# One weight load for a run of matmuls on the same selector, and the diagonal block group by group

One Trainium2 chip, one core. The metric is device time of one execution in microseconds (us), lower is better. "Before" and "after" are the two kernels; a load is a LDWEIGHTS instruction, a burst is PE's work on one strip.

## The reference

```python
B, H, W = 4, 4224, 4224                      # x: fp32, 285 MB
def reference(x):
    ps = np.cumsum(np.cumsum(x, axis=1), axis=2)
    diag = np.diagonal(ps, axis1=1, axis2=2)
    return np.cumsum(diag, axis=1).astype(np.float32)   # (4, 4224)
```

Only the diagonal of the 2D prefix sum is wanted, so each input value has to be read once and added into a few sums.

## The kernel before

Each batch is read in strips of 768 rows, cast to bf16 by the transfer, into three buffers. On a strip, TensorE (PE) sums columns right of the diagonal block, VectorE (DVE) masks the diagonal block and sums rows, ScalarE (ACT) sums the rest of the rows. PE's column sums all go into one tile `d` with a row for each group of 384 columns. A slice of `sel` (128 x 11, one column of ones) as weights, called a selector here, picks the row. A fold (`fold_in`) adds slices of a strip into one tile, with the identity as weights.

```python
def load_rows(o, b, r0):                       # a strip: 12.98 MB of fp32
    nc.gpsimd.dma_start(out=o, in_=x[b, r0 : r0 + f * P, :]...)
def matmul(o, lhsT, rhs, start=False):
    nc.tensor.matmul(o, lhsT=lhsT, rhs=rhs, start=start, stop=False, skip_group_check=True)
def fold_in(o, src, c0, c1, w, start=False):
    for c in range(c0, c1, w):
        matmul(o, ident_h, src[..., c : c + w], start=start and c == c0)
...
def columns(j, lo, hi, rhs):
    k = row_of(j)
    matmul(d[:, lo:hi], sel[:, NG - 1 - k : 2 * NG - 1 - k], rhs, start=first[0])
    first[0] = False
def add_up(strip, f, r0, acc, um, wp=0, ws=None):
    for j in range(g + nw, NG):                # right of the diagonal block
        for q in range(f):
            columns(j, 0, GW, strip[:, q, j * GW : (j + 1) * GW])
    ...
    nc.vector.tensor_mul(out=mu, in0=block, in1=um)
    nc.vector.tensor_sub(out=block, in0=block, in1=mu)
    for q in range(f):                         # the diagonal block: two selectors in turn
        for h in range(nw):
            columns(g + h, 0, GW, mu[:, q, h * GW : (h + 1) * GW])
        if ws > wp:
            act_sum(acc[:, q, 0:1], strip[:, q, wp:ws])
    row_sums(acc[:, :, 1], strip[:, :, ws:hi])
```

The end of the last batch is cut into small transfers, so that little work is left when the last of them lands.

## Time and profile before

| | before |
|---|---|
| time, median of 3 runs | 668.15 us (667.28 to 669.49) |
| span of the profiled run | 665.7 us |
| read from HBM | 285.47 MB, 429 GB/s |
| PE matmuls / weight loads | 981 / 981 |
| busy PE / weight loads / DVE / ACT | 204.5 / 97.8 / 334.6 / 140.3 us |

Busy times of weight loads overlap those of the matmuls (they have a row of their own, PEld). The groups concerned, from the page's part 5 (line, engine, operation, output<-inputs, shapes, count | busy us, mean ns | idle before and what ended it):

```profile
L208 PE MATMUL d<-strip,sel 128*11 128x384 bf16 x603 | 138.7, 403 | 377.7 <-DMA strip<-in_x_dram 377.7
...
L208 PEld LDWEIGHTS <-sel 128*11 128x11 bf16 x849 | 86.2, 102 | 522.3 <-issue 479.3
```

The other lines of before are in the prediction.

### The profile page before, as it was taken

The page shows a single profiled execution, that of the slowest core. Times are in us where ns is not written, and L with a number is a line of the kernel's source. Part 1 is how long each engine was busy: PE and PEld are TensorE (multiplying, and loading weights), DVE is VectorE, ACT ScalarE, POOL GpSimd, SP SyncE. Part 2 cuts the span into 40 slices and gives each one's busy share as a digit, 9 for nine tenths or more (in the row PEclk, how much of TensorE's full clock was granted, in tenths as well). Part 3 has the DMA queues.
Part 4 walks back from the last instruction along what each step waited for, and adds up shares of the span by engine and source line. Part 5 has one row for each costly group of instructions (what it writes and reads, how often), then busy time and mean ns, then how long its engine had stood idle before and what let it go on. Part 6 is the DMA issues. An engine that isn't in the chain of part 4 may idle for free.

```text
span 665.7 us, 2562 instructions
## 1 busy us (share of the span) xinstructions
PE 204.5 (31%) x981; PEld 97.8 (15%) x981; DVE 334.6 (50%) x165; ACT 140.3 (21%) x226; POOL 31.3 (5%) x59
## 2 busy tenths in 40 slices
PE   0081522403117143130221623504032263250427
PEld 0030211101003021110110311202011031120203
DVE  3161625456916153454782524436288343352767
ACT  0001120406300103040630020304063002030436
POOL 7000000000000000000000000000000000001000
PEclk9995857656558585675755957666565586766758
DMA  9999999999999999999999999999999999999998
GB/s 203 219 219 219 219 218 218 219 212 207 220 221 216 219 219 215 219 215 216 212 219 222 218 215 219 216 216 218 216 213 219 221 213 220 216 216 218 218 207 162
DMA packets 7670, 143.23 MB, mean 215 GB/s; under 512 B 702, under 2 KB 1002, under 8 KB 2154
## 3 DMA queue, kind: packets, MB, share of 16 engines
q0 software_dynamic: 7296, 142.47, 99.9%
q1 hardware_dynamic: 362, 0.61, 0.3%
q8 instruction: 7, 0.11, 0.1%
q14 instruction: 5, 0.04, 0.0%
HBM read 285.47 MB, written 0.07 MB: 429 GB/s over the span
## 4 chain that ended last, share of the span: by engine, by line
DVE 47%; another core or an unknown queue 45%; DMA 5%; PE 2%; issue 1%; DVEq 0%; POOLq 0%
DVE acc L230 29%; DVE mu L320 8%; DVE strip L321 8%; DMA strip<-in_x_dram 5%; PE d L208 1%; DVE c L436 1%; PE fold L208 1%; DVE pu L230 0%; DVE c L250 0%; DVE rows L360 0%; DVE acc L335 0%; PE carry_ps L208 0%; DVE pair L239 0%; PE fin L208 0%
## 5 line engine op out<-in xcount | busy, mean ns | idle before, releaser
L208 PE MATMUL d<-strip,sel 128*11 128x384 bf16 x603 | 138.7, 403 | 377.7 <-DMA strip<-in_x_dram 377.7
L225 ACT ACTIVATE dump<-strip 128x416 bf16<-128x416 bf16 (+8 forms) x112 | 128.4, 1146 | 522.0 <-DMA strip<-in_x_dram 519.3
L320 DVE TENSOR_TENSOR mu<-strip,um 128x4608 bf16<-128x4608 bf16 (+1 forms) x24 | 52.4, 2183 | 307.1 <-DMA strip<-in_x_dram 307.0
L230 DVE TENSOR_REDUCE acc<-strip 128x6 f32<-128x4608 bf16 (+6 forms) x23 | 196.0, 8523 | 0.8
L208 PEld LDWEIGHTS <-sel 128*11 128x11 bf16 x849 | 86.2, 102 | 522.3 <-issue 479.3
L208 PE MATMUL d<-mu,sel 128*11 128x384 bf16 x243 | 49.1, 355 | 45.8 <-DVE mu L320 45.8
L321 DVE TENSOR_TENSOR strip<-strip,mu 128x4608 bf16<-128x4608 bf16 (+1 forms) x24 | 52.4, 2183 | 1.0
L76 POOL DMA_DIRECT2D strip<-in_x_dram x24 | 16.4, 686 | 543.0 <-DVE acc L230 281.7
L225 ACT ACTIVATION_READ_ACCUMULATOR dump<-strip 128x1 f32 x112 | 20.9, 186 | 0.0
L208 PE MATMUL d<-ident,rows 128*11 128x128 f32 x24 | 5.2, 379 | 16.8 <-DVE rows L369 16.8
L208 PE MATMUL fold<-strip,ident_h 128*128 128x480 bf16 x8 | 3.4, 598 | 10.7 <-DMA strip<-in_x_dram 10.7
L208 PE MATMUL d<-halves,rows 128*11 128x64 f32 x48 | 5.5, 296 | 0.0
L94 DVE MEMSET um<- 128x4608 bf16 (+1 forms) x2 | 4.9, 2458 | 1.1 <-issue 1.1
L208 PEld LDWEIGHTS d<-ident,rows 128*11 128x11 f32 x24 | 2.6, 119 | 18.5 <-DVE rows L369 11.7
L95 POOL TENSOR_SCALAR_AFFINE_SELECT um<-um 128x4608 bf16<-128x4608 bf16 (+1 forms) x2 | 5.2, 2611 | 2.4 <-DVE um L94 2.4
L208 PEld LDWEIGHTS d<-halves,rows 128*11 128x11 f32 x48 | 5.1, 134 | 1.5 <-issue 1.5
L230 DVE TENSOR_REDUCE pu<-d 11x1 f32<-11x384 f32 x4 | 2.2, 546 | 5.2 <-PE d L208 5.2
L436 DVE TENSOR_TENSOR_SCAN c<-ones_row,carry,c 11x384 f32<-11x384 f32 x4 | 4.0, 1005 | 0.1
L436 DVE TENSOR_TENSOR_SCAN c<-ones_row,carry,d 11x384 f32<-11x384 f32 x4 | 4.0, 1000 | 0.1
L409 POOL DMA_DIRECT2D strip<-in_x_dram x5 | 2.7, 557 | 26.4 <-DMA strip<-in_x_dram 26.4
L208 PEld LDWEIGHTS <-ident_h 128*128 128x128 bf16 x14 | 1.6, 119 | 13.8 <-issue 13.5
L230 DVE TENSOR_REDUCE parts<-strip 128x3 f32<-128x3072 bf16 x1 | 3.4, 3353 | 0.0
(87 smaller groups left out, 37.2 us busy)
## 6 DMA issues: line engine op xcount, KB each, us to landing
strip<-in_x_dram POOLq DMA_DIRECT2D x19, 6336.0 KB, 76.7
strip<-in_x_dram POOLq DMA_DIRECT2D x5, 3168.0 KB, 59.9
strip<-in_x_dram POOLq DMA_DIRECT2D x1, 1080.0 KB, 49.9
strip<-in_x_dram POOLq DMA_DIRECT2D x1, 768.0 KB, 52.9
strip<-in_x_dram POOLq DMA_DIRECT2D x3, 256.0 KB, 54.1
head<-in_x_dram SPq DMA_DIRECT2D x1, 528.0 KB, 4.0
strip<-in_x_dram POOLq DMA_DIRECT2D x1, 192.0 KB, 43.2
strip<-in_x_dram POOLq DMA_DIRECT2D x1, 64.0 KB, 28.6
```

Of the source, the lines that this page charges most:

```text
L76: nc.gpsimd.dma_start(out=o, in_=x[b, r0 : r0 + f * P, :].rearrange("(p f) w -> p f w", f=f))
L94: nc.vector.memset(um, 1.0)
L95: nc.gpsimd.affine_select(out=um, in_=um, compare_op=ALU.is_gt, fill=0.0, base=0, pattern=[[-1, f], [1, f * P]], channel_multiplier=-f,)
L208: nc.tensor.matmul(o, lhsT=lhsT, rhs=rhs, start=start, stop=False, skip_group_check=True)
L225: nc.scalar.activation(out=dump[:, :w], in_=src, func=ACT.Copy, accum_out=acc)
L230: nc.vector.reduce_sum(out=acc, in_=src, axis=AX.X)
L320: nc.vector.tensor_mul(out=mu, in0=block, in1=um)
L321: nc.vector.tensor_sub(out=block, in0=block, in1=mu)
L409: nc.gpsimd.dma_start(out=part_b[:, sb, c0:c1], in_=x[b, r0 : r0 + R, :TB].rearrange("r (k c) -> r k c", k=4)[:, :, c0:c1],)
L436: nc.vector.tensor_tensor_scan(out=c12[:, i, :], data0=ones_row, data1=src, initial=carry[:, i : i + 1], op0=ALU.mult, op1=ALU.add,)
```

## The change

The intent: in a run of matmuls on one selector, or on the identity in the folds, only the first loads the weights, and the others are issued as an instruction that says `ldweights=False`. To have such runs in the diagonal block too, its loops are exchanged: all rows of one column group, then all of the next.

```diff
+    def matmul_on(o, lhsT, rhs):
+        te = nc.tensor
+        te.add_instruction(mybir.InstMatmult(
+            start_tensor_calc=False, stop_tensor_calc=False,
+            tile_position=(0, 0), tile_size=(P, P if lhsT.shape[-1] > 64 else 32),
+            bass_skip_group_check=True, ldweights=False,
+            ...  # name, engine, ins=[rhs, lhsT], outs=[o]
+        ))
     def fold_in(o, src, c0, c1, w, start=False):
         for c in range(c0, c1, w):
-            matmul(o, ident_h, src[..., c : c + w], start=start and c == c0)
+            if c == c0:
+                matmul(o, ident_h, src[..., c : c + w], start=start)
+            else:
+                matmul_on(o, ident_h, src[..., c : c + w])
-        def columns(j, lo, hi, rhs):
+        def columns(j, lo, hi, rhs, same=False):
+            ...
+            if same:
+                matmul_on(d[:, lo:hi], lhsT, rhs)
+                return
@@ add_up @@
-                    columns(j, 0, GW, strip[:, q, j * GW : (j + 1) * GW])
+                    columns(j, 0, GW, strip[:, q, j * GW : (j + 1) * GW], q > 0)
+            for h in range(nw):
+                for q in range(f):
+                    columns(g + h, 0, GW, mu[:, q, h * GW : (h + 1) * GW], q > 0)
             for q in range(f):
-                for h in range(nw):
-                    columns(g + h, 0, GW, mu[:, q, h * GW : (h + 1) * GW])
```

The three matmuls of the last 128 x 128 block get the same treatment (`h > 0`).

More of the change, by code (lines that the diff above doesn't have):

```diff
@@ L210, in matmul @@
         )
+    def matmul_on(o, lhsT, rhs):
+        te = nc.tensor
+        te.add_instruction(
+            mybir.InstMatmult(
+                start_tensor_calc=False,
+                stop_tensor_calc=False,
+                tile_position=(0, 0),
+                tile_size=(P, P if lhsT.shape[-1] > 64 else 32),
+                bass_skip_group_check=True,
+                ldweights=False,
+                name=nc.get_next_instruction_name(),
+                engine=te.engine,
+                ins=[
+                    te.lower_ap(rhs, opt=False),
+                    te.lower_ap(lhsT, opt=False, for_matmul_weights=True),
+                ],
+                outs=[te.lower_ap(o)],
+            )
+        )
     weights4_h = consts.tile([P, P], BF16, name="weights4_h")
@@ L297, in row_of @@
             return (j + t0) % NG
-        def columns(j, lo, hi, rhs):
+        def columns(j, lo, hi, rhs, same=False):
             k = row_of(j)
-            matmul(
-                d[:, lo:hi], sel[:, NG - 1 - k : 2 * NG - 1 - k], rhs, start=first[0]
-            )
+            lhsT = sel[:, NG - 1 - k : 2 * NG - 1 - k]
+            if same:
+                matmul_on(d[:, lo:hi], lhsT, rhs)
+                return
+            matmul(d[:, lo:hi], lhsT, rhs, start=first[0])
             first[0] = False
@@ L353 @@
                 for h in range(3):
-                    columns(LG, h * P, GW, hmu[:, h, : GW - h * P])
+                    columns(LG, h * P, GW, hmu[:, h, : GW - h * P], h > 0)
         a6 = acc6[:, :ns]
```

## The prediction

> **What bounds the kernel now.** I began with the page: busy shares (part 1), the slices (part 2), the bytes (part 3), the chain (part 4).
>
> ```profile
> PE 204.5 (31%) x981; PEld 97.8 (15%) x981; DVE 334.6 (50%) x165; ACT 140.3 (21%) x226; POOL 31.3 (5%) x59
> ...
> PEclk9995857656558585675755957666565586766758
> DMA  9999999999999999999999999999999999999998
> GB/s 203 219 219 219 219 218 218 219 212 207 220 221 216 219 219 215 219 215 216 212 219 222 218 215 219 216 216 218 216 213 219 221 213 220 216 216 218 218 207 162
> ...
> HBM read 285.47 MB, written 0.07 MB: 429 GB/s over the span
> ```
>
> No compute engine is busy more than half of the span. The DMA row is 9 from the first slice to the last, and the rate lies near 217 GB/s throughout (the cast from fp32 to bf16 halves what is counted there; read from HBM it is 429 GB/s). So the kernel is a stream of 285 MB, with a short piece of work behind it. One strip of 768 rows is 768 x 4224 x 4 bytes = 12.98 MB, at 429 GB/s an estimated 30.2 us. The chain of waits shows this beat: the first DVE instruction on a strip starts at 34.8, 64.8, 95.2, 125.1 and 155.0 us. The chain's 45% for "another core or an unknown queue" are the 11 to 20 us gaps between the strips' DVE work, and in the timeline they end with a DMA landing. I read them as waiting for data.
>
> Two places could still be sensitive to PE. The first is the issue of a strip's DMA, which waits until PE, DVE and ACT are through with the old strip in that buffer. The timeline at the end of the first batch, where buffers come free latest:
>
> ```profile
> 174.25 0.71 POOL L76 DMA_DIRECT2D strip<-in_x_dram  x1 [31.27 <-ACT dump L225]
> 183.12 0.71 POOL L76 DMA_DIRECT2D strip<-in_x_dram  x1 [8.16 <-issue]
> ...
> 199.99 2.56 DVE L320 TENSOR_TENSOR mu<-strip,um 128x4608 bf16<-128x4608 bf16 x1 [11.63 <-DMA strip<-in_x_dram]
> ```
>
> The strip that lands at 200 was issued at 142.28. While it streams, the next two are queued at 174.25 and 183.12, so the queue has some 26 us of stock (200 - 174) in its leanest moment. A full strip takes 76.7 us (median) from issue to landing against a beat of 30: it sits in line some 46 us. An issue that comes a few us sooner or later shifts no landing. PE is the last releaser for only 4 of the strip issues (112.2 us of POOL's waiting), and POOL waiting costs nothing while the queue is stocked.
>
> The second place is the end, in the timeline:
>
> ```profile
> 655.80 0.55 DVE L230 TENSOR_REDUCE pu<-d 11x1 f32<-11x384 f32 x1 [0.53 <-PE d L208]
> 661.52 0.46 DVE L239 SCALAR_TENSOR_TENSOR pair<-strip 128x288 f32<-128x288 bf16 x1 [0.85 <-DMA strip<-in_x_dram]
> 662.46 0.39 DVE L239 SCALAR_TENSOR_TENSOR pair<-strip 128x224 f32<-128x224 bf16 x1 [0.15 <-DMA strip<-in_x_dram]
> 662.92 0.50 PE L208 MATMUL fin_e<-weights,esum 128*1 128x32 f32 x6
> 663.50 0.18 DVE L512 TENSOR_TENSOR ye<-fin_e,yl 1x32 f32<-1x32 f32 x1
> ```
>
> DVE waits on PE once (0.53 us at 655.8), but later it stands idle 0.85 us for data at 661.52 and 0.15 us at 662.46. What sets the end is the last landing at about 662.4, then 3.3 us of small work and output (662.4 to 665.7). None of that tail's matmuls is a run on one selector or identity.
>
> **What the Trainium skill says.**
> 1. "TensorE: Matmul & The Clock Gate", section "Step-by-step: what each phase is for": PE pulls a weight load ahead of matmuls in flight, so that the next weights load while the current matmul runs. This trace agrees, in the PEld timeline of a full strip:
>
> ```profile
> 200.28 0.13 PEld L208 LDWEIGHTS <-sel 128*11 128x11 bf16 x1 [0.19 <-issue]
> 200.60 0.13 PEld L208 LDWEIGHTS <-sel 128*11 128x11 bf16 x1 [0.19 <-issue]
> ...
> 203.80 8.78 PEld L208 LDWEIGHTS <-sel 128*11 128x11 bf16 x54 [0.19 <-issue]
> ```
>
> Load and matmul come in pairs every 0.32 us, then 54 of them in 8.78 us, 0.163 us each. The moving operand has 384 columns.
> 2. The same page, "Back-to-back issue gap": a bare matmul of N columns repeats after N/1.2 ns on the half clock, 320 ns here, and N/2.4 + 2.5 ns on the full clock, 162.5 ns. The measured 0.32 and 0.163 us are those of matmuls with no load at all. So, by this comparison, the load is already hidden entirely.
> 3. The same page, "LDWEIGHTS (loading the stationary operand)": columns/1.2 ns, 9 ns for 11 columns. The trace does not agree: 102 ns is the mean of the loads of 11 columns, 119 ns of those of 128. I use the trace.
> 4. "DMA: Bandwidth & Descriptors", "Where 436 GB/s comes from": 435 GB/s as the ceiling of one core's DMA, 425 measured on large transfers. The trace's 429 over the whole span, ramp and tail included, leaves nothing to gain: 285.47 MB at 435 would be 656 us, an estimate.
>
> **The change, part by part.**
> - Runs on one selector: the strip matmuls (603) come six or three to a column group. Counting in the code: a whole batch has 9+7+5+3+1 = 25 groups, the last batch 24 groups of six and 3 of three, so 75 + 27 = 102 loads remain of 603.
> - The diagonal block, now group by group: 11 groups in a whole batch, 10 in the last, 43 loads instead of 243. The reordering is what makes the runs: before, q ran outside and two groups alternated. One DVE instruction produces the whole of mu, so no matmul gets its data later by the new order. ACT's sums keep their order among themselves and do not depend on PE.
> - The small diagonal: 1 load instead of 3. The folds with the identity: 3 instead of 14.
> - Sum: 501 + 200 + 2 + 11 = 714 loads go; PEld falls from 981 to 267 instructions, the total from 2562 to 1848. Busy PEld: 703 x 102 ns = 71.7 us plus 11 x 119 ns = 1.3 us less, from 97.8 to about 25 us.
> - On the path: 73 us lie beside matmuls whose spacing is the bare one, so PE's bursts get shorter by nearly nothing. A full first strip should still take about 13 us for 66 matmuls (200.0 to 212.8). The matmuls number 981 as before.
> - Fetching 714 instructions less: [...]46 KB of 143 MB, 0.2 us of the stream at most.
> Sum on the time: 0 to -0.3 us.
>
> **The rivals.**
> (a) The loads cost PE time and PE gates the issues. Then up to 73 us would go and the time be near 595 us. Against it: the spacing, and a full DMA row. Nothing speaks for it but the x981 in part 1.
> (b) PE's chain before the last scan (eight fold matmuls from 648.89, then d, then the first reduction at 655.80 with its 0.53 us wait) gets 0.5 to 1.5 us shorter, and the tail with it. Some of this may happen, but the two DVE waits on DMA (0.85 and 0.15 us) stand between it and the end: at best -0.3 us, 667.8.
> (c) A wait replaces the one removed: PE's clock. The clock row changes between 5 and 9, and the matmuls go from 0.32 to 0.163 us after some 4 us of work. If the weight loads count as activity, PE without them would stay at half clock longer. At worst a strip's 66 matmuls would take 66 x 0.32 = 21 us instead of 13; 8 us later release against 26 us of stock is hidden. In the tail 0.7 us (fin) and 0.5 us (fin_e) of matmuls would double: +1.2 us, 669.3.
> (d) Matmuls without a load of their own run slower one by one, or the new instruction form carries an extra wait. That too would hide behind the stream up to many us a strip; over 2% slower needs a dry queue in each batch.
>
> **Range and chances.** The center is before's median, 668.15, less 0.15 for (b) and the instruction bytes: 668.0. The three runs before spread from 667.28 to 669.49, and this scatter (0.3%) is larger than any effect I find. Rival (b) takes the low side, (c) the high one: 666.4 to 669.6. Faster by over 2% would need the DMA to move the same bytes at 438 GB/s or more: 1%. Slower by over 2% (13 us) needs the stock to run out: 1%.
>
> **What would show it.** PEld x267 and near 25 us, PE x981 and near 204 us (195 to 210); matmul spacing in a strip still 0.32 and 0.163 us; the DMA row full, 429 GB/s; DVE's starts on the strips every 30 us; the last landing near 662.4, the wait of 0.85 us at the end still there or longer. Wrong would be: gaps in the DMA row that close or open, a beat of strips other than 30 us, PE bursts much shorter (then the load was not hidden, even if the time stays), or a tail after the last landing that differs from 3.3 us by over 1 us.

## The result, and the profile after

| | before | after |
|---|---|---|
| time, median of 6 runs each | 668.47 us | 668.21 us (667.17 to 669.21) |
| ratio after / before | | 0.9998, 95% interval 0.9981 to 1.0014 |
| profiled span | 665.7 us | 666.5 us |
| weight loads | 981 | 981 |

Same time, as predicted. But the page of after, parts 1 to 3 and 5, holds a surprise:

```profile
span 666.5 us, 2562 instructions
...
PE 207.6 (31%) x981; PEld 98.5 (15%) x981; DVE 334.7 (50%) x165; ACT 140.3 (21%) x226; POOL 31.3 (5%) x59
...
DMA  9999999999999999999999999999999999999997
...
HBM read 285.47 MB, written 0.07 MB: 428 GB/s over the span
...
L215 PEld LDWEIGHTS <-sel 128*11 128x11 bf16 x703 | 72.2, 103 | 502.1 <-issue 468.8
...
L208 PEld LDWEIGHTS <-sel 128*11 128x11 bf16 x146 | 14.7, 101 | 18.9 <-issue 10.3
```

The loads are all still there. L215 is the line of the new instruction that should load nothing, and 703 selector loads stand on it (11 more on the identity). The predicted count of 146 on L208 is right, and so is 703 for those that should be gone. The built program's PE order shows the same:

```
1 L208 Ldweights sel
2 L208 Matmult d<-strip,sel 11x384
3 L215 Ldweights sel
4 L215 Matmult d<-strip,sel 11x384
5 L215 Ldweights sel
```

The build puts a load ahead of every bf16 matmul, and in the built program of before every bf16 matmul carries `ldweights: false` as well, each with its load in front. So asking for it changes nothing. Compared instruction by instruction (operands only) in the built programs, after has the same set of 1797 PE instructions as before (871 bf16 matmuls with a load each, and 55 fp32 matmuls), and differs only in the order inside the diagonal blocks. What was measured as "after" is therefore the exchange of two loops, alone.

### The profile page after: what moved, and what is told of

Its sections match the earlier page's. It is cut to its first block, busy times and chain, and to the rows that moved or that the text cites. A ratio compares the mean times of both kernels' runs of the same rounds, so it can differ in the third digit from the quotient of the medians. Undisturbed runs are those within 1.5% of the kernel's fastest.

```text
span 666.5 us, 2562 instructions
## 1 busy us (share of the span) xinstructions
PE 207.6 (31%) x981; PEld 98.5 (15%) x981; DVE 334.7 (50%) x165; ACT 140.3 (21%) x226; POOL 31.3 (5%) x59
## 4 chain that ended last, share of the span: by engine, by line
DVE 48%; another core or an unknown queue 44%; DMA 5%; PE 2%; issue 1%; DVEq 0%; POOLq 0%
DVE acc L254 29%; DVE mu L347 8%; DVE strip L348 8%; DMA strip<-in_x_dram 5%; DVE c L464 1%; PE d L208 1%; DVE parts L254 1%; PE fin L208 1%; DVE pu L254 0%; DVE c L274 0%; DVE acc L363 0%; DVE rows L388 0%; PE carry_ps L208 0%; PE fold L208 0%
## 5 line engine op out<-in xcount | busy, mean ns | idle before, releaser
L208 PE MATMUL d<-strip,sel 128*11 128x384 bf16 x102 | 42.1, 413 | 375.1 <-DMA strip<-in_x_dram 375.1
L215 PEld LDWEIGHTS <-sel 128*11 128x11 bf16 x703 | 72.2, 103 | 502.1 <-issue 468.8
L215 PE MATMUL d<-strip,sel 128*11 128x384 bf16 x501 | 132.1, 407 | 0.0
L215 PE MATMUL d<-mu,sel 128*11 128x384 bf16 x200 | 43.6, 350 | 0.0
L208 PE MATMUL d<-mu,sel 128*11 128x384 bf16 x43 | 15.5, 361 | 45.9 <-DVE mu L347 45.9
L208 PEld LDWEIGHTS <-sel 128*11 128x11 bf16 x146 | 14.7, 101 | 18.9 <-issue 10.3
L208 PE MATMUL d<-ident,rows 128*11 128x128 f32 x24 | 5.2, 379 | 17.5 <-DVE rows L397 16.8
L208 PEld LDWEIGHTS d<-ident,rows 128*11 128x11 f32 x24 | 2.5, 118 | 19.4 <-DVE rows L397 11.7
L208 PE MATMUL d<-halves,rows 128*11 128x64 f32 x48 | 5.3, 290 | 0.0
L208 PEld LDWEIGHTS d<-halves,rows 128*11 128x11 f32 x48 | 4.8, 130 | 1.2 <-issue 1.1
```

The source lines that it names most:

```text
L215: te.add_instruction(mybir.InstMatmult(start_tensor_calc=False, stop_tensor_calc=False, tile_position=(0, 0), tile_size=(P, P if lhsT.shap ...
```

## The experiments

Nine kernels ran in three sets (e1 to e4, e5 and e6, e7 to e9), each set on one chip beside runs of before. My theory: the stream sets the time; and a load was hidden behind the matmul before it anyway. The rivals: loads cost PE time that the stream hides; or loads keep PE's clock up.

### e1: the change as it was meant

The redundant loads are taken out of the built program before it is compiled; the edit checks that the weights held are the same and that the load carries no wait.

```diff
+ON = set()                      # names of the matmul_on instructions
+def drop_loads(nc):
+    for block in nc.main_func.blocks:
+        ...                     # walk PE's code; held = weights of the last kept load
+                if i.name in ON:
+                    assert load.ins[0] == held and not waits(load)
+                    out.add(load.name)
+        block.instructions = [i for i in code if i.name not in out]
     with _tile.TileContext(nc) as tc:
         tile_prefix_sum_2d_diag_kernel(tc, *args)
+    drop_loads(nc)
```

> The changed kernel still shows 981 weight loads: the build puts one ahead of every bf16 matmul, asked for or not. This kernel takes the 714 out after the build, so it is the change as it was meant. Theory (the kernel is a stream, and a load was already hidden behind the matmul before it): weight loads 267, matmuls 981, matmul spacing in a strip still 0.32 us on the slow clock and 0.162 us on the fast one, first strip's 66 matmuls still some 13 us, time within 0.3% of before (666.5 to 669.5). Rival 1 (the loads cost PE time): spacing falls clearly below 0.162 us and the bursts get shorter, the time still same because of the stream. Rival 2 (loads keep the PE clock up): the slow part of each burst grows from some 4 us to over 6 us, the mean granted clock falls below 0.63.

Measured: correct, 668.96 us (6 runs) against 668.17 (11 runs), ratio 1.0002 (0.9984 to 1.0021). The page, part 1, and then PE's timeline in the burst at 200 us (start us, us, what, count):

```profile
span 665.7 us, 1848 instructions
...
PE 205.2 (31%) x981; PEld 24.6 (4%) x267; DVE 334.7 (50%) x165; ACT 140.3 (21%) x226; POOL 31.3 (5%) x59
```

```profile
204.54 0.33 PE L233 MATMUL d<-strip,sel 128*11 128x384 bf16 x1
204.70 0.98 PE L242 MATMUL d<-strip,sel 128*11 128x384 bf16 x5
205.51 0.33 PE L233 MATMUL d<-strip,sel 128*11 128x384 bf16 x1
```

267 loads, 24.6 us of them, 1848 instructions: the prediction's counts, in the kernel that does what it assumed. Six matmuls, only one of them with a load, take 205.51 - 204.54 = 0.97 us, 0.162 us each: the spacing of before. The slow part of that burst lasts from 199.96 to about 203.4, in before from 200.00 to about 203.8, and the mean granted clock is 0.667 (before 0.661). Neither rival shows. PE's busy time did not move (205.2 and 204.5 us).

### e2: twice the matmuls

```diff
+    def again(lo, hi, lhsT, rhs):              # into a scratch tile of PSUM, PE's output memory
+        matmul(extra[:, lo:hi], lhsT, rhs, start=fresh[0]); fresh[0] = False
@@ columns @@
+            again(lo, hi, lhsT, rhs)
```

> Every selector matmul is run twice, the second time into a scratch tile (result stays right). Theory (buffers come free with some 26 us of queued transfers to spare): PE busy near 350 us instead of 208, the first strip's burst near 24 us instead of 13, the DMA row still full, time same within 0.5% (667 to 671; the last d matmuls before the first reduction of the end add up to 1 us). Rival (PE's release of the buffers gates the stream): the time grows by several us for each strip, over 2% in all.

Measured: 669.16 us, ratio 1.001 (0.9991 to 1.0029). PE was busy 344.7 us. The first burst ran from 36.99 to 60.2, 23 us instead of 13, and PE became the last releaser of more buffers. From POOL's timeline:

```profile
222.45 0.72 POOL L76 DMA_DIRECT2D strip<-in_x_dram  x1 [36.99 <-PE extra L208]
```

It comes 21.0 us after its strip's work began (DVE's start at 201.48), in before 11.2 us (211.17 against 199.99): ten us later, at no cost. The profiled span is 2.4 us longer than before's, but the first strip already landed 2.2 us later (37.0 against 34.8); from there to the end it is 631.1 against 630.9 us. The rival (over 2% slower) fell: the stock of queued transfers is real.

### e3 and e4: six times the matmuls, with and without the repeated loads

The same edit with five repetitions, once with the loads that the build adds (e3), once with `drop_loads` (e4). This makes PE the bound, so that a load's cost must show in the time.

> Every selector matmul runs six times (five into scratch), each with its load. PE then has 5076 selector matmuls at 0.162 us = 822 us and must become the bound: first strip lands at 35 us, so 860 to 890 us. Theory: spacing on the fast clock stays 0.162 us with loads. Rival (loads cost time once PE is the bound): spacing above 0.17 us and time over 900 us.

> The same six-fold PE work with the repeated loads taken out after the build (about 150 loads of selectors stay instead of 5076). Here PE is the bound, so a load's cost would show in the time. Theory (a load is hidden entirely behind a 384-column matmul): same time as the six-fold kernel with loads, within 1%. Rival (a load costs its recorded 0.10 us, or a part of it): up to 500 us faster; half hidden, some 250 us faster.

Measured: e3 916.58 us, e4 916.88 us; ratios to before 1.3714 (1.3687 to 1.3740) and 1.3717 (1.3687 to 1.3747). Part 1 of the two pages, e3 first, and then the stretch from 300 to 400 us of each (us, then busy us and count of PE, PEld, DVE, ACT, POOL, granted clock, DMA share, GB/s):

```profile
PE 852.4 (93%) x5226; PEld 462.3 (51%) x5226; DVE 334.2 (37%) x165; ACT 140.2 (15%) x226; POOL 31.4 (3%) x59
```

```profile
PE 853.4 (93%) x5226; PEld 20.8 (2%) x268; DVE 334.2 (37%) x165; ACT 140.2 (15%) x226; POOL 31.4 (3%) x59
```

```profile
300.00:400.00 100.00, 100.00 (x618) 54.48 (x616) 26.54 (x6) 16.81 (x27) 1.43 (x2) 1.00 0.67 141
```

```profile
300.00:400.00 100.00, 100.00 (x617) 1.51 (x17) 26.54 (x6) 18.08 (x29) 1.43 (x2) 1.00 0.68 142
```

4958 loads fewer, 441 us less of recorded load time, and the time is the same to within the noise. PE runs 618 and 617 matmuls in 100 us: 0.162 us each, with or without loads. This is the sharpest test of the step "the load is already hidden entirely", and it held. My absolute figure was too low (860 to 890 us expected): I had summed the 5076 selector matmuls (822 us), while PE was busy 852 us in all, and around it stood the first landing (35 us), waits for DVE (19 us before `mu` and the row sums) and the tail. The rival's "time over 900 us" was met too, but not its cause: the spacing stayed at 0.162 us, and e4 without the loads took as long.

### e5 and e9: three and two loads for each matmul

```diff
+    def more_loads(lhsT):
+        for _ in range(2):                     # e9: range(1)
+            nc.tensor.ldweights(lhsT)
@@ columns @@
+            more_loads(lhsT)                   # ahead of every selector matmul
```

> The changed kernel with two more weight loads of the same selector ahead of every selector matmul: three loads a matmul, where before had one. Asks how much room is left behind a 384-column matmul. If a load occupies what its record says (some 0.09 to 0.10 us), three do not fit into 0.162 us, and the spacing on the fast clock goes to about 0.3 us (0.36 if the two extra ones can't overlap at all). If a load of 11 columns is in truth near 10 ns, it stays at 0.162 us. In both cases the time stays within 0.5% of before, since the longest burst would be 66 x 0.36 = 24 us, as in the kernel with twice the matmuls, which lost nothing.

> Two loads ahead of every selector matmul instead of three or one. With three, the spacing was 0.523 us, and the profile showed no change of clock; the matmuls had the length that elsewhere goes with the slow clock (0.48 us), so I read it as 0.32 us for the matmul and 0.10 us for each load beyond the first. Theory (one load hides, each further one costs 0.10 us): 0.42 us on the slow clock, or 0.26 us if the fast clock is granted. Rival (several loads in a row stop all overlap, so that the number does not matter much): near 0.5 us already with two. Time same as before.

Measured: e5 668.38 us, ratio 1.0016 (0.9993 to 1.0039); e9 668.84 us, one run. The PE timeline of the burst at 200 us, e5 and then e9:

```profile
200.46 2.58 PE L219 MATMUL d<-strip,sel 128*11 128x384 bf16 x5
203.07 0.49 PE L212 MATMUL d<-strip,sel 128*11 128x384 bf16 x1
203.59 2.58 PE L219 MATMUL d<-strip,sel 128*11 128x384 bf16 x5
```

```profile
200.59 2.54 PE L219 MATMUL d<-strip,sel 128*11 128x384 bf16 x5
203.16 0.49 PE L212 MATMUL d<-strip,sel 128*11 128x384 bf16 x1
203.67 2.54 PE L219 MATMUL d<-strip,sel 128*11 128x384 bf16 x5
```

A period of six matmuls is 3.13 us with three loads each (0.52 us per matmul) and 3.08 us with two (0.51 us). Over the longest stretches of equal groups it is 0.523 and 0.514 us. So my theory of e9 (0.10 us for each load beyond the first, 0.42 us) fell and its rival held: a second load in a row costs some 0.19 us over the 0.32 us of the slow clock, the third only some 10 ns more. The PEld timelines, e5 and then e9, show how the loads lie:

```profile
205.05 0.10 PEld L209 LDWEIGHTS <-sel 128*11 128x11 bf16 x2 [0.33 <-issue]
205.16 0.09 PEld L219 LDWEIGHTS <-sel 128*11 128x11 bf16 x1
```

```profile
205.11 0.08 PEld L209 LDWEIGHTS <-sel 128*11 128x11 bf16 x1 [0.33 <-issue]
205.21 0.09 PEld L219 LDWEIGHTS <-sel 128*11 128x11 bf16 x1
```

The two added loads of e5 take 0.10 us together, hardly more than one, and the matmul's own load starts 0.10 to 0.11 us after the first in both kernels. That is about half of the 0.19 us. What the loads wait for, these runs don't show.

There is a side effect on the clock, and because of it neither branch of e5's expectation can be read in the bursts. Up to 653 us they never reached the fast spacing, though PE was busy 430 us in both. Two things show that they ran on the slow clock: their matmuls have the recorded length 0.48 us that elsewhere belongs to slow bursts, and near 655 us, after a dense run of folds (one load each), the spacing drops to 0.36 us in both kernels, with a recorded length of 0.33 us in e5. There the second load costs 0.20 us over the 0.162 us of the fast clock and the third nothing that shows. The clock row of the page reads 9 throughout in both kernels, so it can't be trusted there. Why such a burst doesn't raise the clock stays open.

The time did not notice any of it. The first burst of e5, 66 matmuls, takes 34.5 us (35.2 to 69.7), longer than the 30 us beat of the stream. PE falls behind for three strips, has caught up by the fourth (DVE's start on it at 125.03, in before at 125.11), and the DMA row stays full.

### e6: at which width a load shows

On the idle PE after the first two strips, 32 matmuls with loads and 32 without (`drop_loads`), for widths 32 to 384 and for weights of 11 and of 128 columns.

```diff
+    def widths(lhsT, rhs):                     # rhs: a constant bf16 mask
+        for n in (32, 64, 128, 256, 384):
+            for _ in range(32): nc.tensor.matmul(extra[:m, :n], lhsT=lhsT, rhs=rhs[:, :n], ...)
+            for _ in range(32): matmul_on(extra[:m, :n], lhsT, rhs[:, :n])
```

> The kernel without the 714 loads, and besides, on the idle PE of the first two strips, runs of 32 matmuls of 32, 64, 128, 256 and 384 columns, each with a load of its own and then without, first with 11-column weights, then with 128-column weights. Asks at which width a load starts to show. Theory: at 256 and 384 columns no difference (0.109 and 0.162 us on the fast clock with and without). A load of 0.06 to 0.10 us can't hide behind a matmul of 128 columns or fewer (0.056 us at 128 on the fast clock): there the spacing with loads is that of the load, and without loads it is 1.5 to 3 times smaller. Rival (loads never cost anything): no difference at any width. The time stays same, since this is work for an idle PE.

Measured: correct, 669.57 us in one run. Start to next start in the PE timeline (L289 with loads, L242 without), for weights of 128 columns:

```profile
82.90 0.96 PE L289 MATMUL extra<-um,ident_h 128*128 128x32 bf16 x32
83.72 0.95 PE L242 MATMUL extra<-um,ident_h 128*128 128x32 bf16 x32
84.52 1.09 PE L289 MATMUL extra<-um,ident_h 128*128 128x64 bf16 x32
...
86.38 1.95 PE L289 MATMUL extra<-um,ident_h 128*128 128x128 bf16 x32
88.17 1.95 PE L242 MATMUL extra<-um,ident_h 128*128 128x128 bf16 x32
89.95 3.66 PE L289 MATMUL extra<-um,ident_h 128*128 128x256 bf16 x32
```

At 32 columns 0.82 us for 32 matmuls with loads and 0.80 without: 25.6 and 25.0 ns each. At 128 columns 1.79 and 1.78 us: 56 ns both. With 11-column weights it is the same (0.81 and 0.80 us at 32 columns). My expectation missed: no width of the five shows a load. The rival "loads never cost anything" held for one load between two matmuls. These repeated loads put the same weights back, but different ones fare no worse where the runs have them: before alternated two selectors in its diagonal blocks, and its 12 matmuls there took 2.11 us, (2.11 - 0.33) / 11 = 0.162 us apart. And at the end of before eight matmuls of 128 columns each load another 128 x 128 piece of a strip, (0.62 - 0.22) / 7 = 0.057 us apart (one record is 0.22 us):

```profile
659.00 0.62 PE L208 MATMUL fold<-weights_h,strip 128*128 128x128 bf16 x8 [0.42 <-DMA strip<-in_x_dram]
```

Different weights on matmuls of fewer columns were not tried.

It also corrects how a load's record is to be read. The mean record of these 128-column loads was 97 ns, four times the 25 ns at which they repeated, so it is not the time that PE loses by a load; I read it as a latency. The Trainium skill, "TensorE: Matmul & The Clock Gate", section "Weight-path perf modes — Fast Weight Load (FWL) and DoubleRow", says that full 128-column weights in a type other than fp32 are loaded in four parallel chunks; a load of 128/4 columns at the page's 1.2 per ns is an estimated 27 ns. That agrees with 25.6 ns better than the record does, and better than the gain of about 2 that the same table gives as measured (an estimated 53 ns). But 25.6 ns is also what the matmuls need without loads, so the run only bounds the load.

### e7 and e8: no stream

Only the first three strips are loaded, and every later strip works again on one of these buffers (a wrong result); e8 has the 714 loads taken out besides.

```diff
+    def next_kept():                           # the three buffers in turn
+        turn[0] += 1
+        return kept[(turn[0] - 1) % NBUF]
-            strip = prefetched.pop(0) if prefetched else None
-            if strip is None:
-                strip = strip_tile()
-                load_rows(strip, b, s * F2 * P)
+            strip = next_kept()                # and so for the last strips of each batch
```

> Wrong result on purpose: the changed kernel, but only the first three strips (and the small pieces of the end) are ever loaded; every later strip works again on one of those three buffers. It takes the suspected bound away, and nothing else. Theory (the stream of 285 MB sets the time): the time falls to what the engines need. Three strips land by 95 us as before; VectorE's 335 us of work, of which some 30 us lie before that, and the gaps between its instructions make about 400 to 450 us. Rival (something other than the stream, such as semaphores or the engines' order, sets the beat of 30 us a strip): the time stays over 600 us.

> The same without the stream and without the 714 loads. Asks whether the change would be worth something if the stream did not hide everything. Theory (one load between two matmuls costs no PE time): same time as the kernel without the stream, within 1%. Rival (with PE's work packed closer, the loads cost something): faster by 1 to 15%.

Measured: e7 414.6 us, ratio 0.6207 (0.6195 to 0.6219); e8 415.31 us, ratio 0.6209 (0.6190 to 0.6228). Page of e7, parts 1, 2 and 4:

```profile
PE 192.9 (47%) x981; PEld 95.3 (23%) x981; DVE 333.2 (81%) x165; ACT 140.2 (34%) x226; POOL 17.1 (4%) x38
...
DVE  5306307407999998999999978999999899999995
...
DMA  9999999990000000000000000000000000008600
...
DVE 72%; another core or an unknown queue 9%; PE 9%; DMA 8%; issue 1%; DVEq 0%; POOLq 0%
```

Without the stream DVE is the bound: once the third strip has landed it is busy 294 of the 305 us from 95 to 400, and the kernel takes 62% of the time. So the stream was the bound, and no chain of waits between the engines holds the 30 us beat. And even then removing the loads is worth nothing: e8 is not faster than e7. But this pair is no test of a load's own cost, since PE, busy 47%, stands behind DVE here as it stood behind the stream; that test is e3 against e4. Both landed where expected.

## Why the prediction was right, and where it was wrong

**The time (668.0 predicted, 668.21 measured): right**, for the reason given. The stream sets it: the bytes are the same, 428 GB/s over the span, and the strips' DVE starts in after lie at 35.1, 65.0, 95.2, 125.1 and 155.0 us. e7 shows the bound by taking it away, e2 and e5 the stock by delaying PE. But after, with all its loads, could not test the forecast on loads: that the number fits a kernel other than the one I had in mind is luck, and what confirms the forecast is e1 (668.96, ratio 1.0002).

**"102 loads remain of 603", "PEld falls from 981 to 267 instructions", "about 25 us": the counting was right, the premise wrong.** I took the source's `ldweights=False` for what PE would execute. After has 981 loads, since the build adds one to each bf16 matmul. The counts came true in e1 (267 loads, 24.6 us, 1848 instructions), where the loads were really taken out. The time was right in both, because PE's work is off the path (e2) and the next step holds. Of the bytes saved, 46 KB by the prediction, the page shows 0.11 MB of instructions on queue q8 in before and 0.08 in e1; over a larger difference, e3 against before, 8490 instructions more are 0.56 MB, some 66 bytes each.

**"The load is already hidden entirely": right**, and shown in two ways: the spacing of e1 (0.162 us, as before), and the equal times of e3 and e4 with PE as the bound. The argument in the prediction, a measured spacing compared with that of a bare matmul, was enough to see it.

**"The trace does not agree" on the length of a load: wrong reading.** I set the record of 102 ns against the page's 9 ns for 11 columns, and kept the record. But the record is not what a load costs: e6 repeats a matmul with its 11-column load every 25 ns, so one load occupies 25 ns at most. The third load of e5 adds some 10 ns to e9's two, which agrees with the page's formula (an estimated 9 ns) but is a difference of two profiles on the slow clock. For what a load occupies, the page fits and the record doesn't. The figure was used in the estimate of PEld's busy time, where the record is the right one, and in rival (a), which it made far too large.

**"73 us lie beside matmuls ..., PE's bursts get shorter by nearly nothing": right**, once the loads were really out: PE busy 205.2 us in e1.

**"The reordering" costs nothing: right**; as built, after is this part alone. Its ratio is 0.9998.

**Rival (b), a shorter chain before the last scan: no.** From the first fold matmul to the first reduction over `d` it took 6.91 us in before (648.89 to 655.80), 6.75 in after (648.70 to 655.45) and 6.74 in e1 (648.98 to 655.72). The 0.15 us are there in after too, which has all its loads, so they are not the loads. The prediction also read the end too narrowly: DVE waits on PE twice there, besides the 0.53 us at 655.80 also 0.42 us at 657.24 (for `carry_ps`). Both lie before the last landing.

**Rival (c), PE's clock:** not by the loads. The clock was 0.661, 0.661 and 0.667 in the profiles of before, after and e1. But its tail part did show in after's profiled run:

```profile
660.50 2.15 PE L208 MATMUL fin<-weights,arows 128*1 128x384 f32 x4
...
661.33 0.46 DVE L263 SCALAR_TENSOR_TENSOR pair<-strip 128x288 f32<-128x288 bf16 x1 [0.85 <-DMA strip<-in_x_dram]
...
662.68 0.41 DVE L502 TENSOR_TENSOR yl<-fin,c 1x256 f32<-1x256 f32 x1 [0.89 <-PE fin L208]
```

The same four `fin` matmuls in before:

```profile
660.37 1.24 PE L208 MATMUL fin<-weights,arows 128*1 128x384 f32 x4
```

The wait of 0.85 us for data is still there, as predicted. But the four `fin` matmuls take 2.15 us, in before and e1 1.24, and DVE waits 0.89 us for them, which neither of those has. They are not the ones that the prediction named: the `fin` matmuls on `bsum` (0.71 us) and those on `fin_e` (0.34) are no slower than in before. The granted clock between 655.0 and 661.5 was 0.80 in after and 1.00 in before and e1. So after's tail is not the 3.3 us predicted, but about 4.1 (ACT starts on the last landed piece at 662.36, the span ends at 666.5), and this is the 0.8 us by which its profiled span is longer. e1 lacks the loads and has the fast tail, after has them and the slow one; before has them and the fast one. The profiles of e2, e5, e6 and e9 have 1.24 us too, three of them with all loads or more. So it does not follow the loads. What decides it in one execution is open; 0.8 us is about a third of the spread of the runs of before and after (667.17 to 669.49).

**Rivals (a) and (d): no.** The time neither fell (a) nor did matmuls without a load run slower (d): 0.162 us in e1, and in e6 at every width the same to 1 ns.

## What to carry to other kernels

A busy row of weight loads is no cost in itself: e3 and e4 have 51% and 2% of it and the same time. Compare the start-to-start spacing of the matmuls with that of bare matmuls of the same width; where they agree, as at all five widths of e6, one load per matmul costs nothing. Before crediting an instruction-level change, count its instructions in the built program or in the profile; here the intended saving never reached the chip. And when one engine's work is to be cut, ask first what a delay of that engine costs: doubling PE's work cost nothing here, so a saving there had little to pay in.

## What the Trainium skill lacked or had wrong

- No page says that the build puts a weight load ahead of every bf16 matmul even when the instruction says that it loads none: 981 loads in before and in after, 267 only when they were taken out of the built program.
- "TensorE: Matmul & The Clock Gate", section "Back-to-back issue gap", gives about 81 ns per matmul of 128 columns for a stream of pairs of load and matmul. e6 shows 56 ns with loads (of the same weights) and 56 without, before's eight matmuls with other weights each 57 ns, and e6 109 ns both ways at 256 columns: the page's figure for the bare matmul holds for the pair. At 512 columns, where the sentence has about 131 ns, the matmuls of before onto `fold_a`, with loads, are (0.82 - 0.38) / 2 = 0.22 us apart.
- The same page, "LDWEIGHTS (loading the stationary operand)", doesn't say that the profile's record of a load is something else than columns/1.2: records of 97 ns on average at a repetition of 25.6 ns (128 columns), and about 0.1 us for 11 columns, where a third load in a row added some 10 ns.
- No page says that two loads in a row stop the overlap: spacing 0.514 us with two loads on the slow clock, 0.32 with one, and no fast spacing in such bursts before 653 us though PE was busy 430 of 667 us.
- Neither lacking nor wrong, but easily passed over: "TensorE: Matmul & The Clock Gate", Part 1, calls the clock's trace events unreliable, and this case agrees: in PE's first burst of before (35 to 39 us), and in e5 and e9 throughout, the profile reports a full clock, while the matmuls of the first burst in before were 0.32 us apart and those of e9 only changed pace near 655 us.
